# Two more slots for streamed weights, and small inputs laid out by the host, in a two-layer decoder trunk

## The chip, the cores and the metric

The kernel runs on one core of a Trainium2 chip. The metric is the device time of one execution in microseconds (us); a version's time is the median of its runs. Weights come from HBM by DMA, the work is done by TensorE (PE), VectorE (DVE), ScalarE (ACT) and GpSimd (POOL), and SyncE (SP) issues nearly all DMAs.

## What is computed

Two layers, 256 tokens, width 1024, all in float32. Each layer has a token mixer (three attention branches, gates, one output projection) and a mixture of 32 experts; each is followed by a residual and a LayerNorm with its own gain and bias.

```
for l in range(2):
    mix = token_mixer(x, ...)                 # w_in, w_uq, w_ukv, w_gate, w_a, w_b, w_c, w_o
    x = layer_norm(alpha * x + mix, ln1_g[l], ln1_b[l])
    ffn = hier_moe(x, w_group, b_group, w_sub, b_sub, w1, w3, w2)
    x = layer_norm(alpha * x + ffn, ln2_g[l], ln2_b[l])

hier_moe: top-1 of 4 groups, top-2 of its 8 experts, then
    for e in range(32):
        h = silu(t @ w1[e]) * (t @ w3[e])     # w1[e], w3[e]: 1024 x 256
        y = y + combine[:, e:e+1] * (h @ w2[e])  # w2[e]: 256 x 1024
```

All the weights are read once: 282 MB of HBM reads. The small inputs that the change is about are the norms' gains and biases (`q_norm_g`, `kv_norm_g`, `ln1_g`, `ln1_b`, `ln2_g`, `ln2_b`), the gates' bias `b_gate`, and the router's `w_group`, `w_sub`, `b_group`, `b_sub`.

## The kernel before, in words

**Slots.** Nearly everything large lives in equal slots of 8 KB a partition, 1 MB in all: `NSLOT` (L48) of them, in one pool (`Slots`, L118). A new tile takes the next slot in turn and waits for the last reader of the tile that was there. Working tiles (split weights, attention tiles, gathered rows, the residual) and streamed weights share the slots.

**Ring.** `Ring` (L168) holds the list of all weight loads in the order in which they are used (`plan_weights`, L347). At each release of a slot `pump` (L200) issues loads as long as `fits` (L183) says that the slots will hold them until their last use; for this a dry run of the whole program counts the slots in use beforehand. All the loads go out on SP's queue, in program order (L195, L197). Each load waits on the landing of the load that used its semaphore last (there are eight, in rotation) and on the last reader of its slot.

**Mixer.** The weights of the projections are split into a high and a low part by ACT (L281) and DVE (L282), and multiplied three times (L286 to L288). The mixer is a long run of TensorE work; `mixer` writes the order out from a list, and loads the packed ln1 gains `gpk` (L1331) twelve steps before the output projection.

**Experts.** `moe` works on groups of four experts (Q = 4): eight groups a layer, with e = 0, 4, ..., 28. A group needs twelve loads of 1 MB (four each of w1, w3, w2). The matmuls of w1 and w3 are line L1708, those of w2 L1788, the combination L1774. In layer 0 the small inputs of layer 1 are loaded at the end of the third group (`load_small`, called with e == 2 * Q) and used after the fifth (`small_T`, `small_rows`). The rows of the last norm are loaded in the sixth group (e == NE - 3 * Q, `load_gains` L449) and spread over the partitions in the seventh (`spread_gains`, L455). After the fifth group stands `overflow`, a branch that is not taken here.

**Small inputs.** `load_small` (L401) issues eleven DMAs from POOL's queue: seven rows of vectors into a tile `vec`, of which a transpose makes columns, the router's two matrices, element by element, into part of a slot, and two biases. For layer 0 it is called in `setup` (L337), with POOL's copy of the masks (L343) behind it.

Of the kernel before, what the change touches and what calls it, by code (L numbers as in the profile page):

```python
# [10 lines left out]
F32 = mybir.dt.float32  # L11
# [4 lines left out]
ALU = mybir.AluOpType  # L16
# [3 lines left out]
P = 128  # L20
L = 2
T = 256
NT = 2
D = 1024
KD = 8
# [4 lines left out]
NE = 32  # L30
DE = 256
CAP = 32
Q = 4
# [11 lines left out]

WO = [(0, 512), (512, 256), (768, 256)]

NSLOT = 24  # L48
T1 = 5


# [63 lines left out]
CONSTS, MASKS = constants()  # L115
# [115 lines left out]
class Trunk:  # L231
# [27 lines left out]

    def tap(self, name, ap):  # L260
        if name in self.dbg:
            self.nc.gpsimd.dma_start(self.dbg[name], ap)
# [137 lines left out]

    def load_small(self, l, home, o):  # L401

        nc, a = self.nc, self.a
        v = self.v = self.t([P, P], F32, "vec", 1)
        nc.gpsimd.memset(v, 0.0)
        nc.gpsimd.dma_start(v[0:2], a["q_norm_g"][l].rearrange("(k p) -> k p", p=P))
        nc.gpsimd.dma_start(v[2:3], a["kv_norm_g"][l:l + 1])
        nc.gpsimd.dma_start(v[3:27], a["b_gate"][l].rearrange("(k p) -> k p", p=P))
        nc.gpsimd.dma_start(v[27:35], a["ln1_g"][l].rearrange("(k p) -> k p", p=P))
        nc.gpsimd.dma_start(v[35:43], a["ln1_b"][l].rearrange("(k p) -> k p", p=P))  # L410
        m = max(l - 1, 0)
        nc.gpsimd.dma_start(v[43:51], a["ln2_g"][m].rearrange("(k p) -> k p", p=P))
        nc.gpsimd.dma_start(v[51:59], a["ln2_b"][m].rearrange("(k p) -> k p", p=P))
        self.wgs = home
        self.wgb = home[:, o:o + KD * 72].rearrange("p (k f) -> p k f", k=KD)
        nc.gpsimd.dma_start(self.wgb[:, :, 36:40], a["w_group"][l].rearrange("(k p) f -> p k f", p=P))
        nc.gpsimd.dma_start(self.wgb[:, :, 40:72], a["w_sub"][l].rearrange("(k p) f -> p k f", p=P))
        self.br = self.t([1, 36], F32, "br", 1)
        nc.gpsimd.dma_start(self.br[:, 0:4], a["b_group"][l:l + 1])
        nc.gpsimd.dma_start(self.br[:, 4:36], a["b_sub"][l:l + 1])  # L420

    def small_T(self):

        nc = self.nc
        ps = self.bank()
        nc.tensor.transpose(ps[:, 0:P], self.v, self.ident)
        self.vec = self.t([P, 59], F32, "vecT", 1)
        nc.vector.tensor_copy(self.vec, ps[:, 0:59])
        self.hbg = self.t([P, 24], F32, "hbg", 1)
        nc.vector.tensor_scalar(self.hbg, self.vec[:, 3:27], 0.5, None, op0=ALU.mult)  # L430
        self.wg = self.t([P, KD, 36], F32, "wg", 1)
        w = self.wgb[:, :, 36:72]
        for j in range(2):
            g = self.vec[:, 27 + 8 * j:35 + 8 * j, None].broadcast_to([P, KD, 36])
            nc.gpsimd.tensor_tensor(self.wgb[:, :, 36 * j:36 * j + 36], w, g, op=ALU.mult)
        nc.gpsimd.tensor_copy(self.wg, self.wgb[:, :, 0:36])

    def small_rows(self):

        nc = self.nc  # L440
        ps = self.bank()
        for k in range(KD):
            nc.tensor.matmul(ps[:, 0:72], self.one.broadcast_to([P, P]), self.wgb[:, k], start=k == 0, stop=False)
# [858 lines left out]
    def mixer(self, l, acts):  # L1302
        nc = self.nc
        prep, do = self.prep, self.do
        ps, nfill, n_wo = self.marks
# [10 lines left out]
        for i in range(4, nfill - 4):  # L1316
# [373 lines left out]
    def moe(self, l):  # L1690
        nc = self.nc
# [8 lines left out]
        for e in range(0, NE, Q):  # L1700
# [10 lines left out]
            for c, n in ((0, "w1"), (1, "w3")):  # L1711
                if (e, c) in ((0, 0), (NE - Q, 1)):
                    for k in range(0, KD, 2):
                        w = self.ring.get((l, n, e, k))
# [5 lines left out]
                else:  # L1720
                    w = [self.ring.get((l, n, e + i)) for i in range(Q)]
# [57 lines left out]
            for i, (c0, w) in enumerate(WO if last else ((0, 512), (512, 512))):  # L1779
                n = 1024 // w  # L1780
# [154 lines left out]
def kernel(ctx: ExitStack, tc: tile.TileContext, a, out, dbg=None):  # L1935
# [3 lines left out]
    Trunk(tc, ctx, a, out, dbg, (dry.slots.log, dry.ring.ends)).run()  # L1939


_INS = ["x", "w_in", "q_norm_g", "w_uq", "kv_norm_g", "w_ukv", "w_gate", "b_gate", "w_a", "w_b", "w_c", "w_o",
        "ln1_g", "ln1_b", "w_group", "b_group", "w_sub", "b_sub", "w1", "w3", "w2", "ln2_g", "ln2_b"]


# [17 lines left out]
```

## Time and profile before

| | |
|---|---|
| median of 3 runs | 1004.28 us (1002.66 to 1004.3) |
| the profiled execution | 1004.42 us |
| its span, first to last instruction | 1002.7 us |
| mean granted TensorE clock | 0.954 |
| PE busy | 902.2 us (90% of the span) |
| DVE, ACT, POOL busy | 473.8, 419.0, 165.6 us |
| moved by DMA | 284.76 MB, 284 GB/s in the mean |

The profile is one execution. A page gives the span in 40 slices of 25.07 us; the views of the trace give the same in stretches that one chooses, list who waited for whom, and follow the chain that ended last. "L1708" is a line of the kernel before. Times in the views count from the span's start. The first mixer runs to about 297 us, the first layer's experts to 497, the second mixer to about 790, the second layer's experts to the end.

### The profile page before, as it was taken

Reading aid. Unit: us, or ns where it says so; the run is one execution under the profiler, and the core shown is the slowest. Engines: PE = TensorE matmul, PEld = TensorE weight load, DVE = VectorE, ACT = ScalarE, POOL = GpSimd, SP = SyncE. Lnnn points to the kernel's source line nnn. Section 1 sums busy time; section 2 is a strip of 40 time slices with the busy share of each in tenths; the row PEclk is TensorE's granted clock in tenths of the full one; section 3 lists DMA queues with packets and bytes.
Section 4 is the critical chain, followed back from the end, with each engine's and each line's share of the span. In section 5 each row is a group of like instructions: output and inputs, shape, how many; then the busy total and the mean of one; then the engine's idle time right before and its main releaser. Section 6 shows DMA issues by size and latency. Waiting matters only on the chain.

```text
span 1002.7 us, 18677 instructions
## 1 busy us (share of the span) xinstructions
PE 902.2 (90%) x7584; PEld 706.5 (70%) x7591; DVE 473.8 (47%) x968; ACT 419.0 (42%) x911; POOL 165.6 (17%) x278
## 2 busy tenths in 40 slices
PE   8999999999999966769999999999999997776694
PEld 7888899999985633435489888998999754443251
DVE  5848676945553111111288687676566421100014
ACT  5545555644552301122274646665444632220131
POOL 4531110012100210000035162000451000000001
PEclk9999999999999977789999999999999999987798
DMA  9933171597879999999994044436959899999994
GB/s 330 324 123 126 44 251 43 169 344 244 336 256 404 415 401 419 418 417 396 357 383 139 19 136 149 138 109 217 329 205 401 305 416 417 421 417 419 419 354 150
DMA packets 100170, 284.76 MB, mean 284 GB/s; under 512 B 6324, under 2 KB 53808, under 8 KB 78576
## 3 DMA queue, kind: packets, MB, share of 16 engines
q1 hardware_dynamic: 99088, 283.12, 75.0%
q8 instruction: 62, 1.02, 0.4%
q0 software_dynamic: 992, 0.39, 0.2%
q14 instruction: 28, 0.23, 0.1%
HBM read 282.44 MB, written 1.05 MB: 283 GB/s over the span
## 4 chain that ended last, share of the span: by engine, by line
PE 57%; DMA 25%; issue 8%; POOL 3%; DVE 3%; ACT 2%; SPq 1%; POOLq 0%; DVEq 0%; ACTq 0%
DMA w<-in_w_dram 23%; PE bank L286 12%; PE bank L287 12%; PE bank L288 12%; PE bank L1708 5%; PE bank L840 3%; DMA w<-in_w_in_dram 2%; PE bank L894 2%; PE bank L881 2%; PE bank L1788 2%; PE bank L1667 2%; DVE ws L282 1%; PE bank L843 1%; ACT xp L1443 1%; PE bank L1774 1%
## 5 line engine op out<-in xcount | busy, mean ns | idle before, releaser
L282 DVE TENSOR_TENSOR ws<-w,ws 128x1024 fp32r<-128x1024 f32 (+2 forms) x154 | 190.8, 1248 | 128.3 <-ACT ws L281 123.4
L1708 PE MATMUL bank<-w,xg 128*32 128x256 f32 x2048 | 148.5, 423 | 69.0 <-DMA w<-in_w_dram 59.8
L1708 PEld LDWEIGHTS bank<-w,xg 128*32 128x32 f32 x2048 | 71.0, 121 | 148.3 <-DMA w<-in_w_dram 70.8
L281 ACT ACTIVATE ws<-w 128x1024 fp32r<-128x1024 f32 (+2 forms) x158 | 158.6, 1023 | 35.2 <-PE bank L288 14.4
L286 PE MATMUL bank<-ws,xTh 128*128 128x408 f32 (+3 forms) x320 | 115.9, 362 | 1.2 <-ACT xTh L281 1.2
L286 PE MATMUL bank<-xTh,ws 128*128 128x256 f32 x384 | 111.2, 290 | 0.0
L287 PE MATMUL bank<-ws,xTh 128*128 128x408 f32 (+3 forms) x320 | 110.0, 344 | 1.1 <-POOL ws L282 1.1
L288 PE MATMUL bank<-ws,xTl 128*128 128x408 f32 (+3 forms) x320 | 110.2, 344 | 0.1
L287 PE MATMUL bank<-xTl,ws 128*128 128x256 f32 x384 | 108.6, 283 | 0.0
L288 PE MATMUL bank<-xTh,ws 128*128 128x256 f32 x384 | 108.5, 283 | 0.0
L1738 DVE SCALAR_TENSOR_TENSOR t<-t,cw,bank 128x256 f32<-128x256 f32 x16 | 10.8, 676 | 199.8 <-PE bank L1708 199.8
L1671 ACT ACTIVATE xg<-bank,gpk 128x128 f32<-128x128 f32 x128 | 50.9, 454 | 95.3 <-PE bank L1667 92.7
L286 PEld LDWEIGHTS bank<-xTh,ws 128*128 128x128 f32 x384 | 73.5, 191 | 1.8 <-issue 1.0
L287 PEld LDWEIGHTS bank<-xTl,ws 128*128 128x128 f32 x384 | 73.6, 192 | 0.2
L288 PEld LDWEIGHTS bank<-xTh,ws 128*128 128x128 f32 x384 | 73.5, 191 | 0.0
L1733 ACT ACTIVATE t<-bank 128x256 f32<-128x256 f32 x16 | 6.1, 384 | 146.3 <-PE bank L1708 146.3
L856 ACT ACTIVATE p<-bank,nb 128x128 f32<-128x128 f32 (+1 forms) x92 | 37.3, 420 | 70.0 <-DVE nb L848 65.1
L286 PEld LDWEIGHTS bank<-ws,xTh 128*128 128x128 f32 x320 | 60.9, 190 | 7.7 <-issue 1.7
L1667 PE MATMUL bank<-xg,xp 128*128 128x128 f32 x512 | 63.0, 276 | 2.0 <-ACT xg L1671 2.0
L1667 PEld LDWEIGHTS bank<-xg,xp 128*128 128x128 f32 x512 | 60.6, 192 | 5.9 <-issue 2.5
L287 PEld LDWEIGHTS bank<-ws,xTh 128*128 128x128 f32 x320 | 60.9, 190 | 4.7 <-POOL ws L282 1.4
L288 PEld LDWEIGHTS bank<-ws,xTl 128*128 128x128 f32 x320 | 60.8, 190 | 4.9 <-DVE xTl L282 0.7
(361 smaller groups left out, 1582.2 us busy)
## 6 DMA issues: line engine op xcount, KB each, us to landing
w<-in_w_dram SPq DMA_DIRECT2D x168, 1024.0 KB, 19.0
w<-in_w_gate_dram SPq DMA_DIRECT2D x24, 1024.0 KB, 5.4
w<-in_w_dram SPq DMA_DIRECT2D x80, 256.0 KB, 7.2
w<-in_w_in_dram SPq DMA_DIRECT2D x18, 1024.0 KB, 11.8
w<-in_w_in_dram SPq DMA_DIRECT2D x12, 816.0 KB, 12.8
w<-in_w_o_dram SPq DMA_DIRECT2D x8, 1024.0 KB, 10.0
w<-in_w_a_dram SPq DMA_DIRECT2D x4, 1024.0 KB, 5.4
w<-in_w_c_dram SPq DMA_DIRECT2D x4, 1024.0 KB, 5.3
```

The lines of the kernel that those rows point to most:

```text
L281: self.nc.scalar.activation(hi, src, AF.Copy)
L282: (self.nc.gpsimd if self.lo_pool else self.nc.vector).tensor_tensor(lo, src, hi.bitcast(F32), op=ALU.subtract)
L286: m(out, sh, mh, start=start, stop=False)
L287: m(out, sh, ml, start=False, stop=False)
L288: m(out, sl, mh, start=False, stop=stop)
L840: nc.tensor.matmul(b[:, j * w:(j + 1) * w], q[:, blk * P:(blk + 1) * P], k[:, 0:w], start=j == 0, stop=False)
L856: nc.scalar.activation(p[:, j], v[:, j], AF.Exp, bias=nb[:, j:j + 1], scale=u["scale"], accum_out=sm[:, j:j + 1])
L881: nc.tensor.transpose(ps[:, n * P:(n + 1) * P], p[:, j * P:(j + 1) * P], self.ident)
L894: nc.tensor.matmul(ps[half * 64:(half + 1) * 64, pr * P:(pr + 1) * P], u["v"](u["heads"][pr], kb), u["pt"][:, u["pt0"] + pr * nkb + kb], s ...
L1667: nc.tensor.matmul(ps[:, i * P:(i + 1) * P], self.xn[:, t, k + i], pm[:, t, j:j + Q].rearrange("p e c -> p (e c)"), start=t == 0, stop=t = ...
L1671: nc.scalar.activation(xg[:, k + i], ps[:, i * P:(i + 1) * P], AF.Identity, bias=b, scale=g)
L1708: nc.tensor.matmul(hp[i * CAP:(i + 1) * CAP, c * 256:(c + 1) * 256], xg[:, k, i * CAP:(i + 1) * CAP], w[i], start=k == 0, stop=k == KD - 1 ...
```

## The change

It does five things.

- `NSLOT` goes from 24 to 26, which is 16 KB more a partition. The room comes from the scratch of 16 KB for POOL's DMA descriptors, which is now 64 bytes.
- No DMA is issued by POOL any more.
- The host lays the small inputs out: `vecs` (128 x 164, the rows of `vec` padded to 128 and the two biases behind them), `router` (128 x 288), `gpk` (128 x 16) and `ln2` (one row of 2048) for each layer. `load_small` is two DMAs, on ACT's queue for layer 0 and on SP's for layer 1; `gpk` and the last norm's rows are one DMA each, on SP's queue.
- The router's two copies lie one behind the other instead of interleaved, so POOL multiplies contiguous rows.
- The last norm's rows are loaded in the fourth group (e == 3 * Q) instead of the sixth, so their slot is held two groups longer.

```diff
-NSLOT = 24
+NSLOT = 26
...
     def load_small(self, l, home, o):
-        v = self.v = self.t([P, P], F32, "vec", 1)
-        nc.gpsimd.memset(v, 0.0)
-        nc.gpsimd.dma_start(v[0:2], a["q_norm_g"][l].rearrange("(k p) -> k p", p=P))
...
-        nc.gpsimd.dma_start(self.wgb[:, :, 36:40], a["w_group"][l].rearrange("(k p) f -> p k f", p=P))
-        nc.gpsimd.dma_start(self.wgb[:, :, 40:72], a["w_sub"][l].rearrange("(k p) f -> p k f", p=P))
...
+        eng = nc.sync if l else nc.scalar
+        small = self.t([P, P + 36], F32, "vec", 1)
+        eng.dma_start(small, a["vecs"][l])
+        self.v, self.br = small[:, 0:P], small[0:1, P:P + 36]
         self.wgs = home
+        self.wgb = home[:, o:o + 2 * KD * 36].rearrange("p (j k f) -> p j k f", j=2, k=KD)
+        eng.dma_start(home[:, o + KD * 36:o + 2 * KD * 36], a["router"][l])
...
-    def load_gains(self, l, which, rows=P):
+    def load_gains(self, l):
         gb = self.slots.alloc([P, 2, D], F32, "gb")
-        for j, n in enumerate(("g", "b")):
-            self.nc.gpsimd.dma_start(gb[:rows, j], self.a[f"ln{which}_{n}"][l:l + 1].broadcast_to([rows, D]))
+        self.nc.sync.dma_start(gb[:1], self.a["ln2"][l:l + 1])
...
-                for j, n in enumerate(("ln1_g", "ln1_b")):
-                    nc.gpsimd.dma_start(self.gpk[:, j * KD:(j + 1) * KD], self.a[n][l].rearrange("(p k) -> p k", p=P))
+                nc.sync.dma_start(self.gpk, self.a["gpk"][l])
...
-            if e == NE - 3 * Q:
-                self.gb2 = self.load_gains(l, 2, 1)
+            if e == 3 * Q:
+                self.gb2 = self.load_gains(l)
...
-    nc = _bacc.Bacc("TRN2", target_bir_lowering=False, num_devices=1)
+    nc = _bacc.Bacc("TRN2", target_bir_lowering=False, num_devices=1, dynamic_dma_scratch_size=64)
```

The order of the instructions on PE and DVE stays as it was. These are the places where other engines' order changes.

ACT's queue at the start of the program, before and then with the change (a name after "waits" is a semaphore; DMAHW0 to DMAHW7 are those of the DMAs of SP and ACT):

```order
L1959 UNCONDITIONAL_BRANCH [waits barrier_Pool_Activation_PE_DVE_SP_release]
L1361 ACT_TABLE_LOAD
L1361 ACTIVATE dummy_122<-one 128x1 [waits DVE_49]
L281 ACTIVATE xTh_124<-bank_126 128x4x128 [waits PE_49]
L281 ACTIVATE xTh_124<-bank_133 128x4x128 [waits PE_49]
```

```order
L1962 UNCONDITIONAL_BRANCH [waits barrier_Pool_Activation_PE_DVE_SP_release]
L407 DMA vec_108<-in_vecs_dram 128x164
L411 DMA masks_103<-in_router_dram 128x288 [waits DMAHW0_49]
L1350 ACT_TABLE_LOAD
L1350 ACTIVATE dummy_111<-one 128x1 [waits DVE_49]
L281 ACTIVATE xTh_113<-bank_115 128x4x128 [waits PE_49]
```

Two DMAs now stand ahead of ACT's first instructions, and the second waits on a DMA semaphore. On POOL eleven DMAs and a memset are gone from the same place, so that the copy of the masks is its first instruction.

SP's queue in the first layer's experts, where layer 1's small inputs now stand among the weights (`w`: a 1 MB load), before and then with the change:

```order
L197 DMA w_3955<-in_w_dram 128x2048 [waits DMAHW0_49,PE_49]
L197 DMA w_3957<-in_w_dram 128x2048 [waits DMAHW1_49,PE_49]
L197 DMA w_3959<-in_w_dram 128x2048 [waits DMAHW2_49,PE_49]
L197 DMA w_3961<-in_w_dram 128x2048 [waits DMAHW3_49,PE_49]
L197 DMA w_3997<-in_w_dram 128x2048 [waits DMAHW4_49,PE_49]
```

```order
L197 DMA w_3895<-in_w_dram 128x2048 [waits DMAHW3_49,PE_49]
L197 DMA w_3897<-in_w_dram 128x2048 [waits DMAHW4_49,PE_49]
L407 DMA vec_3900<-in_vecs_dram 128x164 [waits DMAHW5_49]
L411 DMA wr_3899<-in_router_dram 128x288 [waits DMAHW6_49,PE_49]
L197 DMA w_3936<-in_w_dram 128x2048 [waits DMAHW7_49,PE_49]
L197 DMA w_3938<-in_w_dram 128x2048 [waits DMAHW0_49,PE_49]
```

The two new loads take two of the eight DMA semaphores, and the router's waits for a slot (PE_49) ahead of the weights behind it.

The rows of the last norm in layer 0: POOL's queue before, and SP's queue with the change:

```order
L435 TENSOR_TENSOR wr_3907<-wr_3907,vecT_4411 128x8x36 [waits Pool_49]
L436 COPY wg_4415<-wr_3907 128x288
L1658 TENSOR_TENSOR xg_3152<-xg_3152,comb_3098 128x256 [waits DVE_49] x2
L452 DMA gb_4608<-in_ln_g_dram 1x16x64 [waits DMAHW3_49,DMAHW1_49,DMAHW5_49,DMAHW0_49,DMAHW6_49,DMASW0_49,PE_49]
L452 DMA gb_4608<-in_ln_b_dram 1x16x64 [waits DMASW1_49]
```

```order
L197 DMA w_4065<-in_w_dram 128x2048 [waits DMAHW0_49,PE_49]
L197 DMA w_4067<-in_w_dram 128x2048 [waits DMAHW1_49,PE_49]
L442 DMA gb_4069<-in_ln_dram 1x2048 [waits DMAHW2_49,PE_49]
L197 DMA w_4104<-in_w_dram 128x2048 [waits DMAHW3_49,PE_49]
L197 DMA w_4106<-in_w_dram 128x2048 [waits DMAHW4_49,PE_49]
```

Two DMAs leave POOL, and one, which waits for a slot, stands earlier in the program among SP's weight loads. Layer 1 has the same place. `gpk` stands among SP's loads in the same way, with no slot to wait for.

## Rows read from the trace of the kernel before

**Rows 1.** The page, part 2: the span in 40 slices, in tenths.
```profile
PEclk9999999999999977789999999999999999987798
DMA  9933171597879999999994044436959899999994
```

**Rows 2.** Stretches (us): busy time by engine, granted TensorE clock, DMA share, GB/s.
```profile
290.00:300.00 10.00, 8.58 (x93) 7.11 (x96) 4.49 (x32) 9.95 (x25) 1.64 (x4) 1.00 0.69 275
300.00:310.00 10.00, 9.50 (x123) 5.60 (x118) 5.11 (x6) 2.63 (x8) 0.00 (x0) 1.00 0.94 362
310.00:350.00 40.00, 38.84 (x446) 24.05 (x442) 8.28 (x15) 12.88 (x34) 5.04 (x10) 1.00 1.01 416
350.00:360.00 10.00, 3.59 (x26) 0.80 (x18) 1.39 (x2) 1.20 (x2) 2.90 (x4) 0.84 1.02 376
...
452.00:490.00 38.00, 36.85 (x354) 19.07 (x356) 4.87 (x9) 8.24 (x18) 0.00 (x0) 0.90 0.99 377
500.00:530.00 30.00, 26.93 (x138) 25.16 (x138) 26.20 (x55) 20.93 (x44) 11.86 (x14) 0.94 1.00 362
...
790.00:800.00 10.00, 9.35 (x146) 5.70 (x145) 4.54 (x6) 3.64 (x10) 0.68 (x2) 1.00 0.71 259
800.00:845.00 45.00, 43.84 (x478) 26.25 (x478) 10.02 (x16) 15.31 (x40) 1.23 (x2) 1.00 1.01 416
845.00:943.00 98.00, 62.09 (x626) 34.12 (x622) 10.18 (x19) 16.39 (x41) 3.58 (x6) 0.83 1.01 418
```

**Rows 3.** Longest PE waits in 60:350, 300:500 and 790:1003: total us, times, longest.
```profile
PE bank L1708 <- ACT t L1733: 1.7, 3, 0.6
...
PE bank L1708 <- DMA w<-in_w_dram: 27.3, 7, 9.0
...
PE bank L1708 <- DMA w<-in_w_dram: 32.5, 8, 8.3
```

**Rows 4.** Waits of SP's queue: longest in 229:304, two in 330:424, longest in 828:918.
```profile
SPq L197 <- PE bank L288: 27.1, 8, 6.0
...
SPq L197 <- DMA w<-in_w_dram: 76.2, 36, 3.7
SPq L197 <- PE bank L1788: 3.8, 3, 2.9
...
SPq L197 <- DMA w<-in_w_dram: 75.1, 36, 2.4
```

**Rows 5.** The chain that ended last, 800 to 960: start, us, what.
```profile
852.55 19.88 DMA w<-in_w_dram
```

**Rows 6.** Timeline of PE after each layer's last wait: start, us, what [idle before <-releaser].
```profile
452.34 5.34 PE L1708 MATMUL bank<-w,xg 128*32 128x256 f32 x58 [1.45 <-DMA w<-in_w_dram]
...
942.76 5.88 PE L1708 MATMUL bank<-w,xg 128*32 128x256 f32 x58 [1.43 <-DMA w<-in_w_dram]
949.12 3.66 PE L1708 MATMUL bank<-w,xg 128*32 128x256 f32 x64 [0.47 <-ACT t L1733]
```

**Rows 7.** Timeline of POOL: its last early DMA, the masks, layer 1's router.
```profile
8.04 0.54 POOL L420 DMA_DIRECT2D br<-in_b_sub_dram  x1
18.97 1.22 POOL L343 CAST mk<-masks 128x1024 bf16<-128x1024 f32 x1 [10.39 <-DMA masks<-in_masks_dram]
...
412.82 1.42 POOL L435 TENSOR_TENSOR wr<-wr,vecT 128x288 f32<-128x288 f32 x2 [38.49 <-DVE vecT L428]
```

**Rows 8.** The start: PE's transposes of x (timeline), then two stretches as in Rows 2.
```profile
5.62 1.06 PE L522 MATMUL bank<-cst,x 128*128 128x128 f32 x8 [0.80 <-DMA x<-in_x_dram]
...
9.44 1.09 PE L522 MATMUL bank<-cst,x 128*128 128x128 f32 x8 [1.89 <-DMA x<-in_x_dram]
...
4.00:6.00 2.00, 1.20 (x6) 0.41 (x5) 0.00 (x0) 0.00 (x0) 2.00 (x4) 1.00 1.02 365
...
10.00:12.00 2.00, 2.00 (x14) 1.98 (x13) 1.97 (x3) 1.09 (x2) 0.00 (x0) 1.00 1.06 208
```

**Rows 9.** Timeline of ACT at the start.
```profile
0.77 1.28 ACT L1361 ACT_TABLE_LOAD   x1 [0.64 <-PEq L1950]
...
6.28 1.08 ACT L281 ACTIVATE xTh<-bank 128x512 fp32r<-128x512 f32 x2 [4.02 <-PE bank L522]
```

More of the change, by code (lines that the diff above doesn't have):

```diff
@@ L261, in tap @@
         if name in self.dbg:
-            self.nc.gpsimd.dma_start(self.dbg[name], ap)
+            self.nc.sync.dma_start(self.dbg[name], ap)
     def note(self, eng, n, psum=False):
@@ L403, in load_small @@
         nc, a = self.nc, self.a
-        v = self.v = self.t([P, P], F32, "vec", 1)
-        nc.gpsimd.memset(v, 0.0)
-        nc.gpsimd.dma_start(v[0:2], a["q_norm_g"][l].rearrange("(k p) -> k p", p=P))
[L407 to L413, printed above, removed]
-        self.wgs = home
-        self.wgb = home[:, o:o + KD * 72].rearrange("p (k f) -> p k f", k=KD)
-        nc.gpsimd.dma_start(self.wgb[:, :, 36:40], a["w_group"][l].rearrange("(k p) f -> p k f", p=P))
-        nc.gpsimd.dma_start(self.wgb[:, :, 40:72], a["w_sub"][l].rearrange("(k p) f -> p k f", p=P))
-        self.br = self.t([1, 36], F32, "br", 1)
-        nc.gpsimd.dma_start(self.br[:, 0:4], a["b_group"][l:l + 1])
-        nc.gpsimd.dma_start(self.br[:, 4:36], a["b_sub"][l:l + 1])
+        eng = nc.sync if l else nc.scalar
+        small = self.t([P, P + 36], F32, "vec", 1)
+        eng.dma_start(small, a["vecs"][l])
+        self.v, self.br = small[:, 0:P], small[0:1, P:P + 36]
+        self.wgs = home
+        self.wgb = home[:, o:o + 2 * KD * 36].rearrange("p (j k f) -> p j k f", j=2, k=KD)
+        eng.dma_start(home[:, o + KD * 36:o + 2 * KD * 36], a["router"][l])
     def small_T(self):
@@ L431, in small_T @@
         self.wg = self.t([P, KD, 36], F32, "wg", 1)
-        w = self.wgb[:, :, 36:72]
+        w = self.wgb[:, 1]
         for j in range(2):
             g = self.vec[:, 27 + 8 * j:35 + 8 * j, None].broadcast_to([P, KD, 36])
-            nc.gpsimd.tensor_tensor(self.wgb[:, :, 36 * j:36 * j + 36], w, g, op=ALU.mult)
-        nc.gpsimd.tensor_copy(self.wg, self.wgb[:, :, 0:36])
+            nc.gpsimd.tensor_tensor(self.wgb[:, j], w, g, op=ALU.mult)
+        nc.gpsimd.tensor_copy(self.wg, self.wgb[:, 0])
     def small_rows(self):
@@ L442, in small_rows @@
         for k in range(KD):
-            nc.tensor.matmul(ps[:, 0:72], self.one.broadcast_to([P, P]), self.wgb[:, k], start=k == 0, stop=False)
+            nc.tensor.matmul(ps[:, 0:72], self.one.broadcast_to([P, P]), self.wgb[:, :, k], start=k == 0, stop=False)
         nc.tensor.matmul(ps[:, 36:72], self.one[0:1].broadcast_to([1, P]), self.br, start=False, stop=True)
@@ L1939, with laid_out @@
     Trunk(tc, ctx, a, out, dbg, (dry.slots.log, dry.ring.ends)).run()
-_INS = ["x", "w_in", "q_norm_g", "w_uq", "kv_norm_g", "w_ukv", "w_gate", "b_gate", "w_a", "w_b", "w_c", "w_o",
-        "ln1_g", "ln1_b", "w_group", "b_group", "w_sub", "b_sub", "w1", "w3", "w2", "ln2_g", "ln2_b"]
+_INS = ["x", "w_in", "w_uq", "w_ukv", "w_gate", "w_a", "w_b", "w_c", "w_o", "w1", "w3", "w2"]
+def laid_out(a):
+    vecs = np.zeros((L, P, P + 36), np.float32)
+    for l in range(L):
+        m = max(l - 1, 0)
+        rows = [a["q_norm_g"][l], a["kv_norm_g"][l], a["b_gate"][l], a["ln1_g"][l], a["ln1_b"][l], a["ln2_g"][m], a["ln2_b"][m]]
+        v = np.concatenate([r.reshape(-1, P) for r in rows])
+        vecs[l, :len(v), :P] = v
+        vecs[l, 0, P:P + 4], vecs[l, 0, P + 4:] = a["b_group"][l], a["b_sub"][l]
+    router = np.concatenate([a["w_group"], a["w_sub"]], 2).reshape(L, KD, P, 36).transpose(0, 2, 1, 3).reshape(L, P, KD * 36)
+    gpk = np.concatenate([a[n].reshape(L, P, KD) for n in ("ln1_g", "ln1_b")], 2)
+    return {"vecs": vecs, "router": router, "gpk": gpk, "ln2": np.stack([a["ln2_g"], a["ln2_b"]], 1)}
 def kernel(**inputs):
@@ L1948 @@
     from concourse.bass_utils import run_bass_kernel_spmd as _run
-    nc = _bacc.Bacc("TRN2", target_bir_lowering=False, num_devices=1)
+    nc = _bacc.Bacc("TRN2", target_bir_lowering=False, num_devices=1, dynamic_dma_scratch_size=64)
     arrays, args = {}, {}
     feed = {n: inputs[n] for n in _INS}
-    feed["consts"], feed["masks"] = CONSTS, MASKS
+    feed.update(laid_out({n: np.asarray(a) for n, a in inputs.items()}), consts=CONSTS, masks=MASKS)
     for name, v in feed.items():
```

## The prediction

> **What bounds the kernel now.** I read the page's slices first, then stretches of the views around the places where the slices change. TensorE looks like the bound, since it is busy for 90% of the span. But in two places its clock falls while the DMA engines are full [rows 1]: slices 14 to 18 (351 to 476 us) and 33 to 38 (827 to 978 us), the experts' phase of either layer. The stretches say the same: at 350 to 360 PE is busy for 3.59 us of 10 at a DMA share of 1.02, and at 845 to 943 for 62.09 of 98 at 1.01 and 418 GB/s [rows 2].
>
> PE's waits show who holds it. In 60 to 350 no wait on a DMA is among its long ones (the longest group is 0.6 us at most). In 300 to 500 it waits 27.3 us on seven landings of weights, and in 790 to 1003 32.5 us on eight [rows 3]. After the last of these, at 452.34 and at 942.76, PE only runs on what has landed [rows 6]. So two landings, one in each layer, set when everything behind them happens: after the first the rest of layer 0's experts and the second mixer, a long run of PE work in which no load is late (the 32.5 us begin at 845); after the second the end.
>
> What sets those landings? From about 303 us to the last wait of layer 0, and from 800 us to that of layer 1, the transfers run without a gap: shares of 0.94 to 1.02 [rows 2]. In the chain that ended last one load is out for 19.88 us from issue to landing [rows 5] with eight outstanding (there are eight semaphores), which makes 19.88 / 8 = 2.485 us a load, or 422 GB/s for 1 MB; the stretch says 418. In such a run a load lands when the loads before it have landed, and nothing else matters. The last load is therefore early or late by as much as the run began early or late.
>
> And what sets its beginning? Just ahead of it the DMA share is 0.69 at 290 to 300 and 0.71 at 790 to 800 [rows 2]. There SP waits for PE, not for landings: 27.1 us in eight waits on line 288, the last readers of working tiles in slots that a load is to take [rows 4]. From 330 to 424 and from 828 to 918 it is the other way round: 76.2 and 75.1 us in 36 waits on landings, 3.8 us on PE [rows 4]. So slots decide how far ahead the stream is when it becomes continuous, and after that bandwidth decides alone.
>
> **The change part by part.** *26 slots.* With two more slots each load takes the slot that is released two loads earlier in the order. Where slots hold the loads back, before 303 and before 800 us, the stream is then two loads ahead when it becomes continuous. Nothing in the continuous run can give that lead back, since SP waits on landings there. The price of a lead is two landings: 2 x 2.485 = 4.97 us. The last wait of layer 0 ends 4.97 us earlier; the second mixer, which is PE's own, moves up by that; in the slot-bound stretch of layer 1 the loads gain two again relative to PE's work, and its last wait ends earlier by another 4.97 us. That is 9.94 us, and it fits into the waits there are: 27.3 and 32.5 us [rows 3].
>
> *The last norm's rows two groups earlier.* Their slot is gone from the weights for two groups more, so one of the two new slots is not there in that time. It falls into the run in which SP waits 76.2 us on landings and 3.8 on PE [rows 4]. I take no cost; the other bound is one load per layer, 2 x 2.485 = 4.97 us, if the lead shrinks to one load.
>
> *Layer 1's small inputs among layer 0's experts.* They are used after the fifth group and loaded after the third, two groups, or 24 loads of 2.485 us, ahead; a load lands after 19.9 us, so nobody waits for them. What they cost is bandwidth in the continuous run. Before, 350 to 360 us, where POOL's DMAs ran, carries 376 GB/s against 416 just before [rows 2]: 10 x (1 - 376/416) = 1.0 us lost. The new loads are 128 x 164 and 128 x 288 numbers, 0.231 MB, which at 418 GB/s is 0.55 us. That is a gain of 0.5 us (1.0 - 0.55), if the lost rate was theirs. Bounds: all 1.0 us if the new ones cost nothing, and a loss of 1.1 if they run at the rate of the start's small packets, 208 GB/s [rows 8], and the old ones cost nothing. I take 0.5, as the stretch is the place itself. In layer 1 `gpk` and the norm's rows are 16 KB at most: 0.02 us.
>
> *The start.* PE begins its long run at 9.44 us, when the second half of `x` lands [rows 8], and no load holds it after that up to 350 us [rows 3]; so a later `x` moves everything. The 0.231 MB now go out from ACT's queue at once, beside or ahead of `x`: 0.55 us. Before, POOL's small loads were issued until 8.04 us [rows 7], most of their packets coming after `x`, as in 10 to 12 us, where the share is 1.06 and the rate 208 GB/s; at 4 to 6 us the rate is 365 [rows 8], so hardly 0.1 us of what `x` waited for was theirs. I take +0.5 us. Bounds: 0, if the small ones fall into gaps, and +2.8, if they delay `x` as much as 11 small transfers did later: 0.231 MB at 208 GB/s is 1.1 us, twice that for the rows behind it, and the 0.64 us of ACT's first wait [rows 9].
>
> The Trainium skill ("DMA: Bandwidth & Descriptors", section "Issuing engines are not separate DMA queues") says that DMAs of different issuing engines run on the same 16 engines and interleave, so another queue saves only the time of issuing. That speaks against the move to ACT's queue; with the rule the term is the +0.5 taken, and with a queue of ACT's own it would be 0, the time 994.0.
>
> ACT waits at the start too: its table load (1.28 us, at 0.77) and the first copies `xTh` (6.28) now stand behind a DMA that waits on the landing of `vecs`. ACT idles 4.02 us ahead of 6.28 [rows 9], so a landing by about 4.8 us (6.28 less the 1.28 and the dummy's 0.2) is hidden, and 84 KB need 0.2 us of transfer. I take nothing; landing only with the first half of `x`, for which PE waited until 5.62 us [rows 8], it would have `xTh` begin at 7.1, 0.8 us late, which is inside the +2.8 above.
>
> *POOL.* Its copy of the masks at 18.97 waited 10.39 us on the masks' landing, not on its DMAs, and its work on layer 1's router came after 38.49 us of waiting for DVE [rows 7]. So what goes there is off the path: 0. Its contiguous multiplication is 2 x 0.7 us in that same place: 0.
>
> *Order on SP.* SP issues in order, so a small load that waits for a slot holds the weights behind it. The queue of eight outstanding loads covers 19.9 us of that [rows 5]. I take 0 and give the other case a rival.
>
> **The sum**, against the profiled execution's 1004.42 us (0.14 above the median of 1004.28): 1004.42 - 4.97 - 4.97 - 0.5 + 0.5 = **994.5 us**. By the other bounds of the three small terms it lies between 993.5 and 998.4.
>
> The Trainium skill ("HBM Reference", section "Specifications (TRN2)") gives a core's share of the memory as 358 GB/s with both cores of a pair running, and some 425 for one alone. By 358 a load would be 2.93 us and the sum 992.7; the stretches show 416 to 418, so the rate for one alone holds here.
>
> **The rivals.** *A lead of one load only.* The norm's rows hold a slot in the fourth to sixth groups, and the small inputs another; if the lead shrinks to one load per layer, each layer gains 2.49 us and the time is 1004.42 - 4.97 = 999.4. For it: the slots rotate in order, and a slot held longer shifts all behind it. Against it: the 3.8 us of slot waits in the run [rows 4]. Chance 0.12.
>
> *Slots don't decide.* If what starts the continuous run late is not the slots but the order of issue or the eight semaphores, the lead is nought: 1004.4. Against it stand the 27.1 us of slot waits on line 288, with none on landings among the long ones there [rows 4]. Chance 0.05.
>
> *SP stuck behind a small load.* The norm's rows in the fourth group, or the router's, wait for a slot, and twelve loads of a group queue up behind them. The point at which it decides: a wait of over 19.9 us, the loads outstanding [rows 5]; below that it is covered. If SP stood for a whole group, 12 x 2.485 = 29.8 us, the stream would lose 29.8 - 19.9 = 9.9 us in each place; twice for the norm's rows, 19.9, which less the gain of 9.9 is 1014.4. Against it: the weight load behind would otherwise wait for that same slot, as they are given out in turn, and SP's longest wait on PE in the run is 2.9 us [rows 4]. Chance 0.03.
>
> *More than the lead.* After the last wait PE takes 5.34 and 5.88 us for 58 matmuls, when 64 take 3.66 at the full clock a little later [rows 6]. If shorter waits left the clock up, some 2 us a layer would come back: 994.5 - 4 = 990.5. For it: the clock falls to 0.83 in the stretch of waits and is 1.00 where there are none [rows 2]. Against it: most of the waits remain, 22 of 27.3 us. Chance 0.05.
>
> **How the numbers follow.** The forecast has 0.75, the rivals 0.12, 0.05, 0.03 and 0.05. The range runs from the rival with more, 990.5, to that with a lead of one load, 999.5; it takes in the bounds of the small terms, 993.5 to 998.4, and leaves out the two cases without a gain. A measurement of this kernel can tell some 0.2%, 2 us, from no change. Faster by more than that: 0.75 + 0.12 + 0.05 = 0.92; no change 0.05; slower 0.03.
>
> **What would show it right or wrong.** Right: the stretches 290 to 310 and 790 to 800 carry more; the last waits of PE end near 447 and 933 instead of 452.34 and 942.76; its waits on landings are some 22 and 27 us in sum; SP still waits on landings, not on PE, from 330 on. At the start PE's second transposes begin near 9.9, and `xTh` by 6.9 us. With a lead of one load the last waits end near 450 and 938. If slots don't decide, they end where they did. If SP is stuck, it shows a wait on PE of 20 us or more just ahead of line 442 or 411, and a hole in the DMA share behind it. The forecast is wrong, too, if the load that PE waits for last is another one, or if the start moves by more than 2 us.

## The result, and the profile after

The changed kernel takes **989.47 us** (median of 4 runs, 988.87 to 992.32) against 1003.97 (median of 4) in the same comparison: a ratio of **0.9864, 95% interval 0.9843 to 0.9885**. That is faster by 14.5 us, where 9.9 were forecast, and 1.0 us below the range. The profiled execution took 989.41 us with a span of 987.7 us, 15.0 less than before. Runs of one kernel lie several us apart: of 23 runs of the kernel before, taken together, the five of 1007.15 us and more have a mean granted clock of 0.944 to 0.946, the seven below 1002 us one of 0.953 to 0.956.

First the page of the changed kernel, in 40 slices as in [rows 1]:

```profile
PEclk9999999999999997789999999999999999978798
DMA  9943171496888999999996033516949799999994
```

The two places with a low clock under full DMA are still there; that of layer 0 is a slice shorter (three slices below 9 instead of four), that of layer 1 has three as before. The stretches of [rows 2] (the columns are the same):

```profile
290.00:300.00 10.00, 8.58 (x103) 6.81 (x105) 3.77 (x24) 9.57 (x25) 1.41 (x3) 1.00 0.71 255
...
310.00:350.00 40.00, 38.84 (x450) 24.05 (x446) 7.62 (x14) 13.11 (x35) 1.23 (x2) 1.00 1.01 420
350.00:360.00 10.00, 7.47 (x114) 3.43 (x110) 1.38 (x2) 1.31 (x3) 0.00 (x0) 1.00 1.01 420
790.00:800.00 10.00, 10.00 (x94) 5.29 (x87) 5.82 (x9) 3.08 (x7) 0.00 (x0) 1.00 0.96 395
845.00:943.00 98.00, 68.83 (x694) 39.48 (x690) 10.15 (x19) 16.36 (x42) 2.43 (x4) 0.84 1.01 420
```

At 350 to 360 PE is busy for 7.47 us instead of 3.59, and the transfers run at 420 GB/s instead of 376: the first weights are no longer late, and the dip that POOL's loads made is gone. At 790 to 800 the stream is already full (0.96 instead of 0.71). At 290 to 300 it is not (0.71 and 0.69; 255 GB/s instead of 275): the loads of lead were made long before. The first 200 us of the kernel before, of the change, and of the change with 24 slots:

```profile
0.00:200.00 200.00, 194.17 (x1352) 171.97 (x1354) 140.44 (x289) 113.44 (x257) 46.75 (x101) 1.00 0.53 177
```

```profile
0.00:200.00 200.00, 194.46 (x1361) 172.61 (x1362) 141.26 (x289) 114.17 (x257) 40.47 (x89) 1.00 0.55 188
```

```profile
0.00:200.00 200.00, 195.51 (x1369) 173.44 (x1371) 142.04 (x290) 115.25 (x259) 40.63 (x89) 1.00 0.52 178
```

With 26 slots the mean rate is 188 GB/s instead of 177, which makes 2.2 MB in 200 us, two loads; with 24 slots it is 178.

PE's waits for weights in 300:500 and in 790:1003 (us in total, times, longest), which answer to [rows 3]:

```profile
PE bank L1697 <- DMA w<-in_w_dram: 24.0, 7, 9.0
...
PE bank L1697 <- DMA w<-in_w_dram: 27.6, 8, 8.8
```

And those of SP's queue in 330:424, for [rows 4]:

```profile
SPq L197 <- DMA w<-in_w_dram: 65.4, 32, 2.2
...
SPq L197 <- PE bank L1777: 3.2, 2, 2.9
```

27.3 became 24.0, and 32.5 became 27.6. SP still waits on landings (65.4 us) and hardly on slots (3.2). PE's timeline at the start, at the first and last late weights of layer 0, and at the last of layer 1 (start, us, what, idle before and its releaser):

```profile
10.16 1.09 PE L512 MATMUL bank<-cst,x 128*128 128x128 f32 x8 [3.04 <-DMA x<-in_x_dram]
...
353.65 3.64 PE L1697 MATMUL bank<-w,xg 128*32 128x256 f32 x58 [1.83 <-DMA w<-in_w_dram]
...
445.32 5.29 PE L1697 MATMUL bank<-w,xg 128*32 128x256 f32 x58 [1.43 <-DMA w<-in_w_dram]
...
929.55 5.51 PE L1697 MATMUL bank<-w,xg 128*32 128x256 f32 x58 [1.43 <-DMA w<-in_w_dram]
```

The last waits ended at 452.34 and 942.76 before [rows 6]; they end 7.02 and 13.21 us earlier now. The first wait for late weights in each layer stood before at

```profile
357.01 1.06 PE L1708 MATMUL bank<-w,xg 128*32 128x256 f32 x2 [4.48 <-DMA w<-in_w_dram]
...
850.03 1.06 PE L1708 MATMUL bank<-w,xg 128*32 128x256 f32 x2 [4.58 <-DMA w<-in_w_dram]
```

Both became none; in layer 0 the next wait is 1.83.

PE's order is the same in all the kernels here but two, so each of its instructions can be held against itself. This table gives how much later (+) or earlier (-) than in the first profile of before PE starts at the instruction that stood at the given time there, in us:

| kernel | 13 | 60 | 345 | 357 | 452 | 600 | 843 | 850 | 943 | 989 |
|---|---|---|---|---|---|---|---|---|---|---|
| the change | +0.74 | -0.65 | -0.72 | -5.59 | -7.02 | -7.14 | -7.22 | -12.17 | -13.21 | -14.61 |
| the change again | -0.11 | -1.49 | -1.56 | -6.42 | -8.19 | -4.48 | -4.57 | -9.53 | -9.57 | -12.21 |
| 25 slots | -0.16 | -1.55 | -1.61 | -4.93 | -6.18 | -3.45 | -3.58 | -6.96 | -6.25 | -8.57 |
| 24 slots | -0.47 | -1.74 | -1.69 | -1.91 | -3.38 | -3.55 | -3.60 | -4.04 | -3.59 | -6.10 |
| 23 slots | +0.52 | -0.87 | -0.90 | +1.21 | -0.07 | +3.93 | +3.88 | +5.35 | +5.92 | +2.65 |
| start on SP | -0.92 | -2.20 | -2.25 | -7.11 | -8.90 | -8.47 | -8.56 | -13.52 | -13.54 | -13.04 |
| rows in the sixth group | +0.34 | -0.94 | -0.93 | -5.79 | -7.31 | +11.27 | +11.23 | +6.27 | +6.36 | +21.36 |
| rows in the fifth group | +0.17 | -1.22 | -1.32 | -6.18 | -8.30 | -4.27 | -4.37 | -9.33 | -9.55 | -12.19 |
| router in pieces | +0.56 | -0.81 | -0.91 | -5.77 | -6.22 | -6.08 | -6.20 | -11.15 | -10.78 | -10.45 |
| POOL issues, 24 slots | +1.99 | +0.61 | +0.52 | +0.70 | -0.57 | +3.57 | +3.46 | +3.11 | +3.99 | +4.28 |
| before again | -0.08 | -0.81 | -0.88 | -0.69 | -0.73 | -0.75 | -0.82 | -1.01 | +0.13 | -3.08 |

From 345 to 357, and from 843 to 850, stands the lead of the stream: 4.87 and 4.95 us in the change. From 357 to 452 stand the small inputs, from 943 to 989 the tail. With 26 slots, though, PE's marks at 357 and 850 can show little more than the waits of 4.48 and 4.58 us that are gone there; how much earlier the loads land is read from SP, which sends the next load out when an earlier one has landed. The same load in layer 0 and in layer 1, before and then with the change:

```profile
357.03 0.33 SPq L197 DMA_DIRECT2D w<-in_w_dram  x1
...
855.04 0.33 SPq L197 DMA_DIRECT2D w<-in_w_dram  x1
```

```profile
351.18 0.33 SPq L197 DMA_DIRECT2D w<-in_w_dram  x1
...
842.41 0.33 SPq L197 DMA_DIRECT2D w<-in_w_dram  x1
```

It goes out 5.85 and 12.63 us earlier. Less what PE was ahead already (0.72 at 345, 7.22 at 843), the leads are 5.13 and 5.41 us; over the eight profiles with 26 slots they are 5.1 to 5.7 us. "Before again" shows what one profile may differ from another: 0.9 us at the start, and 3.2 in the tail. A profile is not its kernel's median, either: that of 24 slots is of a run of 997.92 us (median 1002.5), that with POOL as issuer of one of 1008.38 (median 1001.3).

### The profile page after: what moved, and what is told of

It reads as the page before. It is cut to its first block, busy times and chain, and to the rows that moved or that the text cites. A ratio compares the mean times of both kernels' runs of the same rounds, so it can differ in the third digit from the quotient of the medians.

```text
span 987.7 us, 18617 instructions
## 1 busy us (share of the span) xinstructions
PE 896.3 (91%) x7584; PEld 706.2 (72%) x7591; DVE 472.1 (48%) x968; ACT 418.6 (42%) x911; POOL 147.9 (15%) x246
## 4 chain that ended last, share of the span: by engine, by line
PE 59%; DMA 24%; issue 7%; POOL 3%; ACT 3%; DVE 2%; SPq 1%; POOLq 0%; DVEq 0%; ACTq 0%
DMA w<-in_w_dram 22%; PE bank L286 12%; PE bank L287 12%; PE bank L288 12%; PE bank L1697 5%; DMA w<-in_w_in_dram 3%; PE bank L830 3%; PE bank L884 2%; PE bank L1777 2%; PE bank L871 2%; PE bank L1656 2%; PE bank L833 1%; PE bank L1763 1%; SPq L197 1%; ACT xp L1432 1%
## 5 line engine op out<-in xcount | busy, mean ns | idle before, releaser
L282 DVE TENSOR_TENSOR ws<-w,ws 128x1024 fp32r<-128x1024 f32 (+2 forms) x154 | 188.9, 1236 | 129.6 <-ACT ws L281 129.0
L1697 PE MATMUL bank<-w,xg 128*32 128x256 f32 x2048 | 145.9, 418 | 60.8 <-DMA w<-in_w_dram 51.6
```

What stands on the lines that cost most here:

```text
L282: (self.nc.gpsimd if self.lo_pool else self.nc.vector).tensor_tensor(lo, src, hi.bitcast(F32), op=ALU.subtract)
L1697: nc.tensor.matmul(hp[i * CAP:(i + 1) * CAP, c * 256:(c + 1) * 256], xg[:, k, i * CAP:(i + 1) * CAP], w[i], start=k == 0, stop=k == KD - 1 ...
```

## The experiments

**How many slots.** Three kernels with the rest of the change:

```diff
-NSLOT = 26
+NSLOT = 24
```

and 25 and 23 in the same way.

> The change with 24 slots instead of 26, all else as in the change. Theory A (two slots are two loads of lead per layer, the rest of the change acts by itself): the two leads that the trace of the change shows are gone (4.87 us in layer 0, 5.41 in layer 1), so 989.5 + 10.3 = 999.8 us, some 4 us faster than the kernel before; PE's first wait on weights in layer 0 ends near 356, and the first mixer still ends 0.7 us earlier than before. Theory B (the slots give one load per layer, the other half comes from the loads that left POOL): 989.5 + 5.0 = 994.5 us. Theory C (the slots give all of the 14.5 us): 1004 us, the small inputs cost and save nothing.

> The change with 25 slots. Theory A: half of what 24 slots cost, one load of 2.49 us per layer, so 989.5 + 5.1 = 994.6 us, half way between the change and the run with 24 slots. Rival (a lead only counts where a release falls at the right place, so the gain comes in steps): equal to the run with 24 slots, or to the change, within 1 us.

> The change with 23 slots, one fewer than before. Theory A (each slot is one load of lead per layer, as long as slots hold the loads before the stream is continuous): one load of 2.49 us per layer behind the run with 24 slots, 1002.5 + 5.0 = 1007.5 us, and PE's waits on weights 2 to 3 us longer in each layer. Rival (from 24 to 26 a threshold was passed, a group of loads that just fits): 1002.5 us as with 24, or a loss of far more than 5 us.

Measured: 24 slots 1002.5 us (ratio to before 0.9981, 0.9961 to 1.0), 25 slots 995.45 (0.9921, 0.9895 to 0.9948), 23 slots 1006.13 (1.0022, 1.0 to 1.0044). PE's first late weights in layer 0 with 23, 24 and 25 slots:

```profile
358.23 1.06 PE L1697 MATMUL bank<-w,xg 128*32 128x256 f32 x2 [6.59 <-DMA w<-in_w_dram]
```

```profile
355.10 0.62 PE L1697 MATMUL bank<-w,xg 128*32 128x256 f32 x2 [4.26 <-DMA w<-in_w_dram]
```

```profile
352.08 0.62 PE L1697 MATMUL bank<-w,xg 128*32 128x256 f32 x2 [1.17 <-DMA w<-in_w_dram]
```

The wait falls by 2.3 and 3.1 us a slot, and with 26 it is gone. The table's leads (357 less 345, 850 less 843) are +2.1 and +1.5 with 23 slots, -0.2 and -0.4 with 24, -3.3 and -3.4 with 25, -4.9 and -5.0 with 26 (-5.1 and -5.4 at SP). From 24 to 26 slots SP gains 4.90 and 4.96 us, two loads in each layer: that is theory A in the trace, and neither B nor a threshold. The medians of 25 and 23 slots lie within 1.4 us of what A gave. That of 24 doesn't: 1002.5 is nearer to C's 1004 than to A's 999.8, though the trace shows the gains at the start and from 357 to 452 that C denies. From 24 to 26 slots the medians move by some 13 us, of which the leads are 9.9 at SP (9.2 at PE's marks); the rest is open.

**The change once more.** No edit.

> The changed kernel itself, on the chip of the next three runs. Theory A (the leads are 10.3 to 10.6 us; what goes beyond is the start, and a clock that after the last wait of a layer falls for one, two or no spells): 988 to 991 us, with runs that lie some 1.7 or 3.4 us apart, and PE at the mark of layer 1's last wait 13 us ahead of the kernel before. Rival (the 14.5 us are in the change itself, each run alike): 989.5 us with all runs within 1 us.

Measured 989.35 us (987.43 to 991.8; ratio 0.9838, 0.9807 to 0.9869). In its profile PE is further ahead at 452 than in the first one, and at 600 it has lost 3.7 us of that. The timeline shows 1.6 us of it, first in the change's first profile, then in this one (with the granted clock of a stretch below):

```profile
464.30 3.69 PE L451 MATMUL bank<-gb,one 1*128 1x512 f32 x8
467.93 5.35 PE L1697 MATMUL bank<-w,xg 128*32 128x256 f32 x64
...
469.20:472.60 3.40, 3.40 (x39) 1.70 (x32) 0.00 (x0) 0.00 (x0) 0.00 (x0) 0.50 0.86 283
```

```profile
463.91 5.01 PE L451 MATMUL bank<-gb,one 1*128 1x512 f32 x8
468.85 5.67 PE L1697 MATMUL bank<-w,xg 128*32 128x256 f32 x64
...
466.20:473.00 6.80, 6.80 (x44) 2.61 (x46) 0.69 (x1) 0.92 (x2) 0.00 (x0) 0.50 0.96 318
```

The eight matmuls that spread the last norm's rows have one row as their weights. Behind them the 64 matmuls that take 3.66 us at the full clock [rows 6] take 5.35 or more: the granted clock is at its lower level (0.5, 1.2 GHz), from 469.2 to 472.6 us in the first profile, which costs 1.7 us, and from 466.2 to 473.0 in the second, where the eight matmuls and the 64 take 3.3 us more than 3.69 and 3.66. The other 2.1 us are lost in the same way, in the 58 matmuls ahead (6.06 us instead of 5.34) and at the start of the second mixer. The table has this in other kernels, too: leaving out the rows in the sixth group, five of its profiles lose 2.7 to 4.1 us from 452 to 600, the other five 0.4 at most. So what theory A says of the clock holds, and the rival doesn't, as the runs lie 4.4 us apart; but of the 13 us that it wanted at the mark of layer 1's last wait only 9.57 are there.

**The last norm's rows later.** The sixth group, where they stood before, and the fifth:

```diff
-            if e == 3 * Q:
+            if e == NE - 3 * Q:
                 self.gb2 = self.load_gains(l)
```

> The change with the last norm's rows loaded in the sixth group again, so that their slot is held by weights for two groups more. Theory A (in the continuous run only bandwidth counts, so a slot more there is worth nothing): 989.5 us, within 0.7. Rival (the rows cost one load of lead in each layer): 989.5 - 5.0 = 984.5 us. Second rival (the rows' load in the sixth group holds SP's queue behind a late release): slower by some us.

> The change with the last norm's rows loaded in the fifth group. In the fourth their load goes out at 397 us, in the sixth at 472, behind the weights that stand before it, and PE, which wants them at 464, waited 13.8 us. Theory A (only the landing before the use counts): between the two the load goes out near 442 and lands 20 us later, at 462, so no wait, or one of up to 2 us: 989.4 to 992 us. Rival (each group later costs its part): half of what the sixth cost, 1007 us.

Measured: the sixth group 1024.87 us (1.0197, 1.0166 to 1.0228), the fifth 991.75 (0.989, 0.9863 to 0.9916). For the sixth, the timeline of SP's queue:

```profile
472.19 0.45 SPq L442 DMA_DIRECT2D gb<-in_ln_dram  x1
```

and that of PE:

```profile
478.48 7.16 PE L451 MATMUL bank<-gb,one 1*128 1x512 f32 x8 [13.83 <-DMA gb<-in_ln_dram]
```

The load stands in SP's order behind the weights of the last group, goes out at 472.19, and PE waits 13.83 us for 8 KB, with the clock down afterwards (the eight matmuls take 7.16 us instead of 3.69); in layer 1 the same, with 13.08 us. The two waits are 26.9 of the 35.4 us by which this kernel is slower than the change. In the fifth group the load goes out at 434.14, and PE doesn't wait, as theory A has it; the rival's 1007 us is out. In the sum I had a small load holding up weights in mind; here the weights hold up the small load. Of the second rival only the sign came true: SP's longest wait on PE in 400 to 500 is 2.9 us, so the rows' load didn't hold up the queue. The move from the sixth group to the fourth, which I had priced as a possible loss, is what lets these rows go by SP without a wait. That it costs nothing itself is also seen: from 357 to 452, where their load stands in the fourth group, PE gains 1.47 us on before with 24 slots, no less than the change (1.43), and 1.52 with the rows in the sixth group.

**The small loads.** Layer 1's router from the original arrays (in runs of 16 and 128 bytes), by SP:

```diff
-        eng.dma_start(home[:, o + KD * 36:o + 2 * KD * 36], a["router"][l])
+        if l:
+            for n, f, w in (("w_group", 0, 4), ("w_sub", 4, 32)):
+                eng.dma_start(self.wgb[:, 1, :, f:f + w], a[n][l].rearrange("(k p) f -> p k f", p=P))
+        else:
+            eng.dma_start(home[:, o + KD * 36:o + 2 * KD * 36], a["router"][l])
...
```

and the host's layout, issued by POOL, with 24 slots:

```diff
-NSLOT = 26
+NSLOT = 24
...
-        eng = nc.sync if l else nc.scalar
+        eng = nc.gpsimd
...
-        self.nc.sync.dma_start(gb[:1], self.a["ln2"][l:l + 1])
+        self.nc.gpsimd.dma_start(gb[:1], self.a["ln2"][l:l + 1])
...
-                nc.sync.dma_start(self.gpk, self.a["gpk"][l])
+                nc.gpsimd.dma_start(self.gpk, self.a["gpk"][l])
...
```

> The change with layer 1's two router matrices loaded from the original arrays as before (runs of 16 and 128 bytes), but from SP's queue. Theory A (the form of the transfer costs the bandwidth, whoever issues it): the stream of layer 0 loses the 1.6 us that the step at 357 us showed before, instead of 0.6, so 1.0 us slower than the change; the shift shows in one load's landing behind the router. Rival (the cost was POOL's queue): within 0.3 us of the change at layer 0's last wait.

> 24 slots, the host's layout, and all small loads issued by POOL (with its 16 KB for descriptors). To be held against the run with 24 slots and SP and ACT as issuers. Theory A (who issues doesn't matter): 1002.5 us, within 1 us of that run, and the same shifts at layer 0's waits. Rival (POOL's issuing is what cost the time before): 1004 us or more, with a start up to 1 us later, as POOL's first work and the landing of x stand behind it.

Measured: in pieces 993.64 us (0.989, 0.9856 to 0.9924), POOL as issuer 1001.3 (0.9973, 0.9944 to 1.0003). From the 357 to the 452 mark the kernel in pieces gains 0.45 us on before, POOL with the host's layout 1.27, the change 1.43 and 1.77, 24 slots 1.47. So in the stream the form is worth some 1.0 to 1.3 us, and who issues hardly 0.2, as theory A has it. At the start it is otherwise: with POOL as issuer PE is 0.5 us behind before at the 345 mark, where ACT's kernels are 0.7 to 1.7 ahead. That is the rival's later start; its 1004 us isn't reached. In pieces the issue itself is dear on SP (timeline, then the stretch behind it):

```profile
372.93 9.38 SPq L413 DMA_DIRECT2D wr<-in_w_sub_dram  x1
```

```profile
380.00:390.00 10.00, 7.68 (x66) 3.05 (x66) 0.00 (x0) 0.38 (x1) 0.00 (x0) 0.60 0.90 296
```

POOL had issued the same in 0.91 us. SP needs 9.38, and at 380 to 390 the stream falls to 296 GB/s; in the change it is 413 there. Of the 4.3 us that the medians lie apart (1.0 was forecast) the trace places about 1 at the last wait of layer 0; the rest isn't settled.

**The start.** Layer 0's small loads behind the masks on SP:

```diff
-        eng = nc.sync if l else nc.scalar
+        eng = nc.sync
```

> The change with layer 0's two small loads on SP's queue, behind the masks, instead of at the head of ACT's. Theory A (at the start PE hangs on the second half of x alone): its transposes begin near 9.4 instead of 10.16 us, and the whole moves by that: 988.8 us. Rival (the first 47 us are set by POOL's chain, which ends at the landing of the masks and not at x): no change, 989.5 us, PE 0.7 us earlier at 10 us and equal at 50.

Measured 990.74 us (0.986, 0.983 to 0.989). The second transposes begin at 8.51 us instead of 10.16, and PE is 2.25 us ahead of before at 345; 0.7 to 1.5 more than the change. At the mark of 60 it is 0.7 to 1.6 ahead of the change still, so the rival's "equal at 50" is out. Theory A holds in the trace; the median doesn't show it, with runs from 987.51 to 992.67 us.

**Before again.** No edit.

> The kernel before, for a second profile. Theory A (the 1.3 us by which PE gains between 13 and 60 us in every kernel with the host's layout is in the program, and the clock after the last waits is not): at 48 us PE waits 1.3 us on POOL again; the stream's step of some 4 us at 357 us is there again; the tail's landings and the clock may differ by up to 3.4 us. Rival (these are one execution's accidents): the wait at 48 us or the step at 357 us is gone.

Measured 1003.19 us (1.001, 0.9987 to 1.0032). The step at 357 us is there again: 4.10 us between two loads of SP, where the others are 2.49. The wait for POOL at 48 us isn't; another of 1.3 us, on line 752, is. PE's waits for POOL in 14 to 60 us, in the first profile of before, in the second, and in the change:

```profile
PE bank L1015 <- POOL cs L990: 1.3, 1, 1.3
PE bank L826 <- POOL qn L752: 0.6, 2, 0.5
```

```profile
PE bank L826 <- POOL qn L752: 1.3, 2, 1.2
```

```profile
PE bank L816 <- POOL qn L742: 0.9, 2, 0.7
```

So theory A has the step, and the rival is right for the start: PE gains 0.73 us on the first profile between 13 and 60, without any edit. And in the tail, PE's weight loads waited 2.9 us for the last w2 in the first profile of before:

```profile
PEld bank L1788 <- DMA w<-in_w_dram: 2.9, 4, 1.2
```

In the second no such wait is among the long ones, and PE gains 3.2 us on the first in the tail. So some 3 us of the 15.0 between the first two profiles were the tail of one execution. The second profiles of both kernels have spans of 999.6 and 990.0 us, 9.6 apart, the change's with the 3.7 us lost behind 452.

**Spreading the rows a group earlier,** alone, and with the start on SP:

```diff
+            if e == NE - 3 * Q:
+                self.spread_gains(self.gb2)
             if e == NE - 2 * Q:
-                self.spread_gains(self.gb2)
...
```

> The change with the spreading of the last norm's rows (eight matmuls, 3.69 us of PE) at the end of the sixth group instead of the seventh: there PE then waits some 9 us for weights anyway. Theory A (it moves from behind the last wait, where PE sets the pace, into a wait, and with it the place where the clock falls): layer 0 gains 3.7 us and up to 1.7 for the clock; in layer 1 the landing of the last w2 comes at most 1 us before its use, so hardly 1 us: 984 to 986 us. Rival (the clock falls in the tail anyway, and the rows have not landed yet by the sixth group): 989 to 995 us.

> The change with layer 0's small loads on SP behind the masks and the rows spread in the sixth group. Theory A (the start gains 0.7 us, and the tail, where the landing of the last w2 now sets the end, nothing): 988.5 us, hardly to be told from 989.4. Rival (the two add up, 0.7 and 3.7 us for layer 0): 985 us.

Measured: alone 989.34 us (0.9847, 0.9815 to 0.988), both 987.91 (987.08 to 989.23; 0.9855, 0.9838 to 0.9873). Once it has risen after the last waits, the clock stays up to the end of the experts in both layers of both profiles, and the 3.7 us of work are gone from there. In layer 0 the gain is in the trace: at the mark of 600 PE is 9.07 and 8.98 us ahead of the first profile of before, in the change's two profiles 7.14 and 4.48. In layer 1 it turns into a wait. PE's weight loads behind its last wait, with both edits:

```profile
PEld bank L1777 <- DMA w<-in_w_dram: 3.0, 4, 1.2
```

PE now catches up with the last w2, as it did in the first profile of before. Alone, the edit has a profile with a span of 984.9 us, of the run of 987.56, but its median misses theory A's 984 to 986; it lies in the rival's range, though neither of the rival's reasons holds: the clock stays up, and the rows have landed by the sixth group, as the eight matmuls don't wait. Why the median shows nothing of layer 0's gain is open. For both edits theory A's 988.5 fits, and the rival's 985 doesn't. The version with both edits has the lowest median, 1.4 us below the change, but the intervals overlap: it beats the kernel before, and isn't told apart from the change.

## Why the prediction was wrong

*The step that failed* is the sum of the small terms. It has -0.5 us for the inputs, +0.5 for the start and nothing for layer 1's stream and the tails, so nothing together. The runs show some -1.2 for the inputs, about -0.8 for the start, and in the first two profiles 1.8 us more behind the last wait of layer 1, which the second profiles of both kernels do not repeat. The path and the leads, 9.94 us of the 9.9 forecast, held.

*What bounds the kernel, and the lead of two loads:* right. The forecast was 4.97 us a layer; SP's issues show 5.13 and 5.41, 5.41 and 5.49 in the repeat, and the runs with 23 to 25 slots show the steps between. One sign did not come: 290 to 310 us carries no more than before (255 and 366 GB/s instead of 275 and 362), as the two loads are ahead by 200 us already. The stream kept the lead through the continuous run, as SP went on waiting on landings. The rates of the stretches, 420 GB/s, agree with the 425 or so that the Trainium skill ("HBM Reference", section "Specifications (TRN2)") gives for a core alone.

*The rows held two groups longer:* right that they cost no lead. What was missed is what they gain: on SP's queue the place of before costs 13.83 and 13.08 us of wait.

*Layer 1's small inputs, among layer 0's experts:* mis-sized. The term was -0.5 us; at PE's marks 1.43 and 1.77 were measured, of which some 0.3 and 0.6 belong to the lead, since SP's load of 357.03 goes out 5.85 and 6.97 us earlier, and PE's mark at 357 is only 5.59 and 6.42 ahead. So about 1.2 is theirs. I read the loss of before from a stretch of 10 us that ended in the middle of it (1.0 us); the one step of 4.11 us against 2.49 is 1.6. What the new loads cost was nearly right: two landings there are 3.15 us apart in the change, so 0.66 is lost, where 0.55 was forecast.

*The start:* the sign was wrong. The term was +0.5 us; from +0.74 at 13 us PE came to -0.65 at 60, and the kernels of the change with ACT as the issuer lie 0.7 to 1.7 us ahead of the first profile of before at 345. The `x` landing was later in the first profile, as forecast (10.16 instead of 9.44), but over the nine profiles with ACT as issuer the mark at 13 goes from -0.47 to +0.74. And the stretch from 33 to 50 us hangs on POOL's chain in part (PE waits 1.9 us for it before and 0.9 in the change), which I had taken off the path by looking at two of its places only. The profile of before again is 0.88 ahead too, so about half is one execution's.

*Layer 1's stream and the tails:* 0 was forecast. From 850 to 943 the change gained 1.0 us, half of it lead that the mark at 850 could not show, the repeat none. Behind the last wait I had PE "only run on what has landed". It doesn't always: the tail is set by PE or by the last w2, whichever is later, and the clock falls in between. I had read PE's waits, not those of its weight loads, where the 2.9 us stood.

*The sum:* 5.13 + 5.41 for the leads, 1.2 for the inputs and about 0.8 for the start (the mean of nine profiles against two) make 12.5 of the 14.5 us. The other 2.0 aren't settled; candidates are fewer or shorter spells of the low clock in the tails, which one profile per kernel can't count. The bounds of the small terms left 1.0 us downward (993.5) and 3.9 upward; they are those of the inputs and the start, and the third, the rows' 4.97, is in the rival of 999.4 only. So terms that each came out about 1 us better had no room.

*The rivals:* the one of 990.5 is nearest to the measured time, but not by its mechanism. It wanted some 2 us a layer from a clock that stays up after shorter waits; the 58 matmuls behind the last waits take 5.29 and 5.51 us instead of 5.34 and 5.88, 0.4 us in all. Of the others none came: the lead is two loads, and SP's longest wait on PE in 330 to 424 is 2.9 us.

Of the signs, `xTh` began at 5.86 us, inside what I gave. POOL as issuer of the same transfer gave 1.27 us from 357 to 452, and SP 1.47, both with 24 slots. That agrees with the rule of the Trainium skill ("DMA: Bandwidth & Descriptors", section "Issuing engines are not separate DMA queues") that another queue saves only the time of issuing. That time is not always small: for the transfer in pieces it was 9.38 us on SP and 0.91 on POOL.

## What to carry to other kernels

Where a stretch is bound by bandwidth, its end is set by how far ahead the stream is when the stretch begins: count the loads by which a buffer more lets it start, and multiply by the time of one load; that gave 4.97 us here, and 5.1 to 5.7 were measured. Read such a lead where the loads are issued or land: at the consumer it can't show more than the wait that was there. A small load on a queue of large ones has to be placed by when it goes out, not by when it is needed: the router's 144 KB landed 15.6 us after their issue on SP's queue, behind the weights, and 6.6 us after it on POOL's. And read the waits of the weight loads, and a second profile of the same kernel, before a term of 1 us is put on anything: tails and starts differ by 1 to 4 us from one execution to the next.

## What the runs showed that was not expected

- A DMA of 1024 runs of 128 bytes took SP 9.38 us to issue, POOL 0.91 us.
- After eight matmuls with one row of weights (3.69 us, or 4.74 to 5.01 where the clock falls within them) the 64 that follow take 5.35 to 5.94 us instead of 3.66, in layer 0 of all the eleven profiles in which they stand behind the last wait and don't wait themselves; where they stood a group earlier, the clock stayed up behind the last wait. In layer 1 the same 64 take 3.66 us in six of these eleven, so the eight matmuls alone don't decide it; what does is open.
- POOL's small operations of 0.2 us take about 1 us at some places (on line 750 before, 0.99 us at 42.05 and 0.20 at 46.33), and the places differ from kernel to kernel. No run tries why, but the traces show them beside an operation of VectorE's (L282 splits weights; its two inputs lie in slots):

```profile
41.99 0.99 DVE L282 TENSOR_TENSOR ws<-w,ws 128x816 fp32r<-128x816 f32 x1
...
42.05 0.99 POOL L750 TENSOR_TENSOR t<-cs,cst 128x8 f32<-128x8 f32 x1
...
46.33 0.20 POOL L750 TENSOR_TENSOR t<-cs,cst 128x8 f32<-128x8 f32 x1
```

Of POOL's 218 TENSOR_TENSORs in the first profile of before, 35 take over 0.4 us more than the shortest of their form, and all the 35 overlap a TENSOR_TENSOR of VectorE's. Of the 139 that overlap none, none is long; 44 overlap one and are not long. The other profiles show the same, with 36 long ones each. That this moves the end of POOL's chain at the start, and with it PE, is likely but not shown.
